# Layer 1's values as seven products of quarters, computed between key units 6 and 7

## The chip, the cores and the metric

One NeuronCore of a Trainium2 chip runs the whole kernel. The metric is the device time of one execution in microseconds (us), as a median of runs. TensorE (PE in the profile) multiplies matrices, VectorE (DVE), ScalarE (ACT) and GpSimd (POOL) work elementwise, SyncE (SP) issues most of the transfers, GpSimd the adding ones. Sixteen DMA engines carry the transfers of all queues.

## The reference

A two-layer decoder step: layer 0 is gated linear attention, layer 1 differential attention, each with an MLP. The prompt has 16 meta tokens and 1024 further ones, width 1024; beside it, 8 running sequences with 4096 past tokens each attend to a paged cache of keys and values. What the change touches is the projection of layer 1, `x @ w_in`, split into queries, keys and values:

```python
def diff_project(x, w_in, pos):
    B, T, _ = x.shape
    nq = DIFF_HEADS * 2 * DIFF_DH
    q, k, v = jnp.split(x @ w_in, [nq, 2 * nq], axis=-1)
    q = rope_partial(q.reshape(B, T, DIFF_HEADS, 2, DIFF_DH), pos)
    k = rope_partial(k.reshape(B, T, DIFF_HEADS, 2, DIFF_DH), pos)
    v = v.reshape(B, T, DIFF_HEADS, DIFF_DV)
    return q, k, v
```

Queries, keys and values have 1024 columns each. The values `v` of the prompt are an output (`v_rows_p`), and the attention reads them.

## The kernel before

Every large product is made of three matmuls in fp32r (`mm3`, L205 to L208): each operand is kept as a high part (`whi`, `XH`, cast by ScalarE) and a low part (`wlo`, `XL`, the difference, by GpSimd for weights in L194 and by VectorE for tokens in L203), and high x high, high x low and low x high are summed in one PSUM bank. The tokens lie transposed in `XH`/`XL`: halves `c` of 512 tokens, blocks `k` of 128 inner columns (eight of them, so a half of the inner size is four blocks).

The projection of layer 1 (loop at L1237) runs over 12 units `u` of 256 output columns (0 to 3 queries, 4 to 7 keys, 8 to 11 values) and, in each, over 4 steps `t2_` of two blocks of 128 tokens. A step is 48 matmuls of 256 columns into one bank (`mmt`); ScalarE copies the bank to `qo` (L1252), VectorE turns the first 16 of every 64 columns for queries and keys (L1260 to L1263), SyncE stores the result (L1269). The weights of a unit come through two `raw` buffers of 128 x 512 and two pairs of `whi`/`wlo` (pools `wrp` and `wsp`, two buffers each).

Woven into the same stretch is the paged decode of the 8 running sequences (generator `decode`): for each sequence 32 pages of keys and, one sequence later, 32 pages of values of 512 KB each through 10 buffers `pg`. Key pages are multiplied by the query (L942, three of four on VectorE and one on GpSimd) and summed (L943); value pages are multiplied on TensorE (L983, eight records a page). The softmax of a sequence (`soft`, from L948) stands between its key pages and its value pages; `v_end` (L994 to L999) ends it.

Between the units stand side steps: after unit 3 and unit 6 the residual `Y` (128 x 8192, one bank of on-chip memory for 1024 tokens) is scaled and gets its bias row (`alpha_row`, L1130 and L1128) and is stored to `xres`, after which `Y` is free; after unit 9 the keys and queries of the first two heads are loaded (`load_qk`), and `prep(0)` transposes them in the middle of the last unit, for the attention that follows.

Code is recorded in program order, and a scheduler then orders each engine's instructions by that order as a priority and by its own model of when an operand is ready; on the chip, each engine and each queue runs its list in order. `decode` has the lowest priority. `issue_after` ties an instruction behind another.

Layer 1's MLP, later in the kernel, already computes products by seven products of quarters (`UP_*`, `DOWN_*`); weight sums there are made by adding transfers from GpSimd's queue (L1620), on buffers `RW`.

## Time and profile before

| | us |
|---|---|
| median of 3 runs | 2798.05 |
| lowest and highest | 2793.52, 2802.12 |
| the profiled execution's own time | 2807.25 |
| its span, first to last instruction | 2805.4 |
| granted TensorE clock, mean | 0.991 |

| engine | busy, us | share of the span |
|---|---|---|
| PE | 2725.4 | 97% |
| PEld (weight load of TensorE) | 2237.5 | 80% |
| DVE | 1935.9 | 69% |
| ACT | 1107.1 | 39% |
| POOL | 1091.0 | 39% |

All traces are of one profiled execution. In a row of the time line stand the start, the duration, the engine, the line, the operation, out<-in with shapes, and in brackets the idle time before it and what ended that. A group's row has the line, engine, operation, out<-in, count, busy us and mean ns of one, then the engine's idle time before them. Matmuls overlap, so the time of one is read from the distance of starts, not from its duration.

### The profile page before, as it was taken

The page shows a single profiled execution, that of the slowest core. Times are in us where ns is not written, and L with a number is a line of the kernel's source. Part 1 is how long each engine was busy: PE and PEld are TensorE (multiplying, and loading weights), DVE is VectorE, ACT ScalarE, POOL GpSimd, SP SyncE. Part 2 cuts the span into 40 slices and gives each one's busy share as a digit, 9 for nine tenths or more (in the row PEclk, how much of TensorE's full clock was granted, in tenths as well). Part 3 has the DMA queues.
Part 4 walks back from the last instruction along what each step waited for, and adds up shares of the span by engine and source line. Part 5 has one row for each costly group of instructions (what it writes and reads, how often), then busy time and mean ns, then how long its engine had stood idle before and what let it go on. Part 6 is the DMA issues. An engine that isn't in the chain of part 4 may idle for free.

```text
span 2805.4 us, 52242 instructions
## 1 busy us (share of the span) xinstructions
PE 2725.4 (97%) x19849; PEld 2237.5 (80%) x19849; DVE 1935.9 (69%) x3011; ACT 1107.1 (39%) x2266; POOL 1091.0 (39%) x744
## 2 busy tenths in 40 slices
PE   8989999999999999999999999899999999999997
PEld 5867767987777777777798989777899889798985
DVE  5375363678787787777667730887647888978698
ACT  4324463152221222221242112777526546355553
POOL 2132112234344443434234312200026667686765
PEclk9999999999999999999999999999999999999999
DMA  7475545735798898888658995212044555564674
GB/s 237 164 242 207 202 154 184 262 97 184 284 333 320 310 351 302 331 319 306 250 173 312 363 368 169 64 55 79 31 126 90 103 139 113 134 133 104 140 179 112
DMA packets 275624, 562.81 MB, mean 201 GB/s; under 512 B 23510, under 2 KB 144412, under 8 KB 271276
## 3 DMA queue, kind: packets, MB, share of 16 engines
q1 hardware_dynamic: 256076, 522.75, 54.0%
q0 software_dynamic: 19296, 36.71, 8.1%
q8 instruction: 156, 2.56, 0.4%
q14 instruction: 96, 0.79, 0.1%
HBM read 533.00 MB, written 29.52 MB: 201 GB/s over the span
## 4 chain that ended last, share of the span: by engine, by line
PE 78%; DVE 9%; DMA 4%; ACT 4%; issue 3%; POOL 1%; SPq 0%; DVEq 0%; POOLq 0%; ACTq 0%
PE mmt L206 18%; PE mmt L207 18%; PE mmt L208 18%; PE smt L983 4%; PE axt L206 3%; PE axt L208 3%; PE axt L207 3%; PE smt L1359 2%; ACT as L1337 1%; DMA swt<-in_mlp_w 1%; DVE pg L942 1%; PE prt L1333 1%; PE axt L1354 1%; DVE XH L203 1%; DVE sc L943 1%
## 5 line engine op out<-in xcount | busy, mean ns | idle before, releaser
L194 POOL TENSOR_TENSOR wlo<-raw,whi 128x512 fp32r<-128x512 f32 x252 | 361.5, 1448 | 719.0 <-ACT whi L193 616.2
L206 PE MATMUL mmt<-whi,XH 128*128 128x256 f32 (+1 forms) x1760 | 524.2, 300 | 1.1 <-DVE ast L1335 0.9
L207 PE MATMUL mmt<-wlo,XH 128*128 128x256 f32 (+1 forms) x1760 | 522.8, 298 | 0.6 <-POOL wlo L194 0.6
L206 PE MATMUL mmt<-XH,whi 128*128 128x512 f32 (+1 forms) x1216 | 435.9, 360 | 3.4 <-DVE HL L203 1.8
L208 PE MATMUL mmt<-whi,XL 128*128 128x256 f32 x1536 | 432.6, 285 | 0.0
L208 PE MATMUL mmt<-XH,wlo 128*128 128x512 f32 (+1 forms) x1216 | 432.4, 356 | 0.2 <-POOL wlo L1622 0.2
L193 ACT CAST whi<-raw 128x512 fp32r<-128x512 f32 x252 | 150.4, 619 | 574.2 <-DMA raw<-in_mlp_w 172.9
L206 PEld LDWEIGHTS mmt<-whi,XH 128*128 128x128 f32 x1760 | 330.8, 189 | 39.6 <-issue 24.3
L943 DVE TENSOR_REDUCE sc<-pg 128x16 f32<-128x1024 f32 x256 | 308.2, 1211 | 69.7 <-POOL pg L942 67.2
L207 PEld LDWEIGHTS mmt<-wlo,XH 128*128 128x128 f32 x1760 | 332.6, 189 | 16.8 <-issue 5.8
L942 DVE TENSOR_TENSOR pg<-pg,qb 128x1024 f32<-128x1024 f32 x192 | 267.1, 1398 | 63.5 <-DMA pg<-in_cache_k 50.5
L207 PE MATMUL mmt<-XL,whi 128*128 128x512 f32 x768 | 306.7, 400 | 0.0
L208 PEld LDWEIGHTS mmt<-whi,XL 128*128 128x128 f32 x1536 | 288.6, 189 | 7.3 <-issue 6.8
L206 PEld LDWEIGHTS mmt<-XH,whi 128*128 128x128 f32 x1216 | 229.6, 189 | 46.9 <-issue 7.6
L942 POOL TENSOR_TENSOR pg<-pg,qb 128x1024 f32<-128x1024 f32 x64 | 163.0, 2548 | 249.3 <-DMA pg<-in_cache_k 139.8
L208 PEld LDWEIGHTS mmt<-XH,wlo 128*128 128x128 f32 x1216 | 229.9, 189 | 36.1 <-issue 3.3
L206 PE MATMUL mmt<-whi,HH 128*128 128x512 f32 x512 | 204.8, 401 | 5.6 <-DVE Y L1172 3.7
L208 PE MATMUL mmt<-whi,HL 128*128 128x512 f32 x512 | 203.9, 398 | 0.0
L207 PE MATMUL mmt<-wlo,HH 128*128 128x512 f32 x512 | 203.4, 397 | 0.0
L1622 POOL TENSOR_TENSOR wlo<-rw,whi 128x512 fp32r<-128x512 f32 x92 | 154.4, 1737 | 93.6 <-ACT whi L1621 90.4
L1622 POOL TENSOR_TENSOR wlo<-RW,whi 128x512 fp32r<-128x512 f32 x96 | 164.1, 1750 | 59.1 <-ACT whi L1621 59.0
L207 PEld LDWEIGHTS mmt<-XL,whi 128*128 128x128 f32 x768 | 145.3, 189 | 39.3 <-issue 8.0
(438 smaller groups left out, 5697.6 us busy)
## 6 DMA issues: line engine op xcount, KB each, us to landing
pg<-in_cache_k SPq DMA_DIRECT2D x256, 512.0 KB
pg<-in_cache_v SPq DMA_DIRECT2D x256, 512.0 KB
raw<-in_mlp_w SPq DMA_DIRECT2D x164, 256.0 KB
swt<-in_mlp_w SPq DMA_DIRECT2D x32, 1024.0 KB
rw<-in_mlp_w SPq DMA_DIRECT2D x116, 256.0 KB
RW<-in_mlp_w POOLq DMA_DIRECT2D x96, 256.0 KB, 5.7
swt<-in_gla_w_in SPq DMA_DIRECT2D x12, 1024.0 KB
swt<-in_diff_w_in SPq DMA_DIRECT2D x12, 1024.0 KB
```

The lines of the kernel that those rows point to most:

```text
L193: S.copy(hi[:, c], raw)
L194: G.tensor_tensor(lo[:, c], raw, hi[:, c].bitcast(F32), op=ALU.subtract)
L203: return eng.tensor_tensor(lo, src, hi.bitcast(F32), op=ALU.subtract)
L206: TE.matmul(ps, ah, bh, start=first, stop=False)
L207: TE.matmul(ps, ah, bl, start=False, stop=False)
L208: return TE.matmul(ps, al, bh, start=False, stop=last)
L942: eng.tensor_tensor(pg, pg, qb, op=ALU.mult)
L943: return V.tensor_reduce(sc[:, n, :], pg.rearrange("p (h d) -> p h d", d=64), op=ALU.add, axis=AX.X).ins
L983: m = TE.matmul(acc[i * TS : i * TS + 16, :256], w[r, n, :], pg[r, i * 256 : (i + 1) * 256], start=n == 0, stop=n == NPG).ins
L1333: TE.matmul(pss[m], qs[i][r, ts_], ks[j][r, x:y], start=i + j == 0, stop=i == 1)
L1359: TE.matmul(out, at, v, start=j == 0, stop=j == t + 1)
L1622: G.tensor_tensor(lo[:, k, :], t, hi[:, k, :].bitcast(F32), op=ALU.subtract)
```

## The change

The loop over units ends at 8. The values are computed by `v_rows`, which runs between unit 6 and unit 7, as seven products of quarters: tokens by halves `c` and inner size by halves `k`, weights by halves `k` and halves `u` of the 1024 value columns, each quarter 512 x 512. In the order 5, 1, 6, 2, 3, 4, 7 (`V_SEQ`), with A(c,k) for tokens and W(k,u) for weights, the factors are:

| product | tokens | weights |
|---|---|---|
| 5 | A(1,0) - A(1,1) | W(0,0) + W(0,1) |
| 1 | A(0,0) | W(0,0) |
| 6 | A(0,0) - the sum of 5 | the sum of 5 + W(1,1) |
| 2 | A(0,1) | W(1,0) |
| 3 | A(0,1) - the sum of 6 | W(1,1) |
| 4 | A(1,1) | the sum of 6 + W(1,0) |
| 7 | A(1,0) - A(0,0) | W(1,1) + W(0,1) |

A product is 4 tiles of 128 tokens, each 12 matmuls of 512 columns, alternately in banks `axt` and `mmt`. Token sums are formed by VectorE in a quarter of `Y` (`VX`) and split into one buffer `vtok`; weight sums are formed in another quarter of `Y` (`VW`), where a plain load is followed by an adding transfer, or an adding transfer goes onto the sum that stands there. The other two quarters of `Y` (`VA`, `VB`) hold running results. Product 1's result is stored, and product 2's is added onto it in DRAM by an adding store. The operands of a product are recorded after two tiles of the one before; those of product 5 after step 0 of unit 6 (`v_first`).

So that `Y` is free in time, the bias rows and the store to `xres` move from after unit 6 to after unit 4. The loads of the first two heads' keys and queries move from after unit 9 to behind the values, since `vtok` takes the place of their buffers; `prep(0)` stays in the middle of the last unit, which is now key unit 7.

```diff
-    rqp = er.enter_context(tc.tile_pool(name="rqp", bufs=2, side="right"))
+    vs = ExitStack()
+    vtok = vs.enter_context(tc.tile_pool(name="vtok", bufs=1, side="right")).tile([P, 2, 4, 512], F32R, name="vtok")
...
+    V_SEQ = (5, 1, 6, 2, 3, 4, 7)
+    VX, VW, VA, VB = (Y[:, 2048 * i : 2048 * (i + 1)].rearrange("p (k n) -> p k n", n=512) for i in range(4))
...
+        for j in (0, 2):
+            b = slice(j, j + 2)
...
+            if rest == ["run"]:
+                V.tensor_tensor(x, hi, x, op=ALU.subtract)
+                V.tensor_tensor(x, x, lo, op=ALU.add)
+            else:
+                h2, l2 = at(*rest[0])
+                V.tensor_tensor(x, hi, h2, op=ALU.subtract)
+                V.tensor_tensor(x, x, lo, op=ALU.add)
+                V.tensor_tensor(x, x, l2, op=ALU.subtract)
+            split(vtok[:, 0, b], vtok[:, 1, b], x)
...
+        for k in range(4):
...
+            t = VW[:, k] if len(terms) > 1 else wrp.tile([P, 512], F32, name="raw")
+            for q in terms:
+                if q != "run":
+                    if q == terms[0]:
+                        dma(t, src(q))
+                    else:
+                        nc.gpsimd.dma_start(t, src(q), accum_op=ALU.add)
+            S.copy(hi[:, k], t)
+            G.tensor_tensor(lo[:, k], t, hi[:, k].bitcast(F32), op=ALU.subtract)
...
+        for k in range(4):
+            mm3(ps, ah[:, k, ts_], al[:, k, ts_], bh[:, k], bl[:, k], k == 0, k == 3)
+        if i == 5:
+            S.copy(VB[:, t], ps)
+        elif i == 1:
+            S.copy(VA[:, t], ps)
+            dma(v_out(0, t, 0), VA[:, t])
+        elif i == 6:
+            V.tensor_tensor(ps, ps, VA[:, t], op=ALU.subtract)
+            V.tensor_tensor(VB[:, t], VB[:, t], ps, op=ALU.add)
+            S.copy(VA[:, t], ps)
+        elif i == 4:
+            V.tensor_tensor(VA[:, t], ps, VA[:, t], op=ALU.subtract)
+        else:
...
+            if i == 2:
+                S.copy(o, ps)
+                nc.gpsimd.dma_start(v_out(0, t, 0), o, accum_op=ALU.add)
+                return
+            V.tensor_tensor(o, ps, VB[:, t], op=ALU.add)
+            dma(v_out(int(i == 7), t, 1), o)
...
-    for u, t2_ in ((u, t) for u in range(12) for t in range(4)):
+    for u, t2_ in ((u, t) for u in range(8) for t in range(4)):
+        if (u, t2_) == (7, 0):
+            v_rows(v_now)
+            vs.close()
+            rqp = er.enter_context(tc.tile_pool(name="rqp", bufs=2, side="right"))
+            raws = [load_qk(0), load_qk(1)]
...
-        if (u, t2_) == (11, 2):
+        if (u, t2_) == (7, 2):
...
-        elif (u, t2_) == (6, 3):
+        elif (u, t2_) == (4, 3):
...
-        elif (u, t2_) == (9, 3):
-            raws = [load_qk(0), load_qk(1)]
+        elif (u, t2_) == (6, 0):
+            v_now = v_first()
```

Three places of the engines' lists. First SyncE, where the residual's store (`xres<-Y`, four pieces) frees `Y`. Before, its first two pieces in unit 7 (`L1123` loads rows of a bias, `L909` is a page's address):

```order
L1269 DMA out_k_rows_p<-qo 128x2x256
L909 TENSOR_LOAD ptab
L909 ISA x2
L1278 DMA xres<-Y 128x8x256
L1123 DMA ht<-in_ln_mlp_b 128x256
L1278 DMA xres<-Y 128x8x256
```

Now, in units 5 and 6, with product 5's four weight slabs (`Y<-in_diff_w_in`): around the third and fourth piece of the store, and then between unit 6's second and third store of keys:

```order
L1372 DMA xres<-Y 128x8x256
L1272 DMA Y<-in_diff_w_in 128x512
L1363 DMA out_k_rows_p<-qo 128x2x256
L1272 DMA Y<-in_diff_w_in 128x512
L1372 DMA xres<-Y 128x8x256
L1363 DMA out_k_rows_p<-qo 128x2x256
```

```order
L911 DMA pg<-in_cache_k 128x1024
L909 TENSOR_LOAD ptab
L909 ISA x2
L1363 DMA out_k_rows_p<-qo 128x2x256
L1272 DMA Y<-in_diff_w_in 128x512 x2
L1363 DMA out_k_rows_p<-qo 128x2x256
```

Two slabs (those whose columns of `Y` the first two pieces of the store cover, 0 and 2) are loaded right behind the third piece, the other two half a unit later. Before, the store stood two units later and nothing was loaded into `Y` behind it.

Second GpSimd, from the end of unit 6 to the last key page. `L942` is a page's product, `L974` and `L992` memsets of the decode, `wlo` a weight's low part. Before, with key unit 7's weights and the first of the values':

```order
L942 TENSOR_TENSOR pg<-pg,qb 128x1024
L194 TENSOR_TENSOR wlo<-raw,whi 128x512 x2
L942 TENSOR_TENSOR pg<-pg,qb 128x1024
L194 TENSOR_TENSOR wlo<-raw,whi 128x512
L974 MEMSET pg 32x1024
L194 TENSOR_TENSOR wlo<-raw,whi 128x512
L992 MEMSET pg 128x256
L942 TENSOR_TENSOR pg<-pg,qb 128x1024
L194 TENSOR_TENSOR wlo<-raw,whi 128x512 x6
```

Now, in one run (`wlo<-Y` are the slabs of a weight sum, for products 5 and then 6; `wlo<-raw` those of product 1; L1274 the adding transfers):

```order
L1274 DMA Y<-in_diff_w_in 128x512 x2
L942 TENSOR_TENSOR pg<-pg,qb 128x1024
L1276 TENSOR_TENSOR wlo<-Y,whi 128x512
L1276 TENSOR_TENSOR wlo<-raw,whi 128x512 x2
L1274 DMA Y<-in_diff_w_in 128x512 x2
L1276 TENSOR_TENSOR wlo<-Y,whi 128x512
L1274 DMA Y<-in_diff_w_in 128x512
L942 TENSOR_TENSOR pg<-pg,qb 128x1024
L1274 DMA Y<-in_diff_w_in 128x512
```

```order
L974 MEMSET pg 32x1024
L992 MEMSET pg 128x256
L1276 TENSOR_TENSOR wlo<-raw,whi 128x512 x2
L1276 TENSOR_TENSOR wlo<-Y,whi 128x512
L1274 DMA Y<-in_diff_w_in 128x512
L1276 TENSOR_TENSOR wlo<-Y,whi 128x512
L1274 DMA Y<-in_diff_w_in 128x512
L942 TENSOR_TENSOR pg<-pg,qb 128x1024
L1276 TENSOR_TENSOR wlo<-Y,whi 128x512 x2
```

Between the last three page products of the decode there now stand 8 low parts and 6 adding transfers, where 4 low parts stood.

Third VectorE, at the last key page (`L943` its sum, `L948` the first step of the softmax) and at the decode's end (`L999`). Before, behind the last rotation of key unit 7:

```order
L1263 TENSOR_TENSOR qo<-qo,qr 128x8x16
L943 TENSOR_REDUCE sc<-pg 128x16
L948 TENSOR_REDUCE mx<-sc 128x16
L999 COPY oT<-smt 128x4 x2
L952 TENSOR_REDUCE m_18529<-smt 16x1
```

Now, first at the last key page (`vtok` is product 6's token split), then at the decode's end (L1305 and L1309 are results of products 3 and 7, L1298 of product 4):

```order
L942 TENSOR_TENSOR pg<-pg,qb 128x1024
L943 TENSOR_REDUCE sc<-pg 128x16 x2
L948 TENSOR_REDUCE mx<-sc 128x16
L203 TENSOR_TENSOR vtok<-Y,vtok 128x1024
L1252 TENSOR_TENSOR Y<-XH_85,Y 128x1024
L203 TENSOR_TENSOR vtok<-Y,vtok 128x1024
```

```order
L1305 TENSOR_TENSOR qo<-mmt,Y 128x512
L999 COPY oT<-smt 128x4 x2
L1388 MEMSET cmask 128x320
L1480 TENSOR_TENSOR zoq<-oT 128x64
L1483 TENSOR_SCALAR zoq<-smt 128x64
L1305 TENSOR_TENSOR qo<-axt,Y 128x512
L1309 TENSOR_TENSOR qo<-Y,axt 128x512
L1305 TENSOR_TENSOR qo<-mmt,Y 128x512
```

Product 6's tokens stand behind the last key page, and product 7's results behind the last step of the decode.

More of the change, by code (lines that the diff above doesn't have):

```diff
@@ new lines, in v_weights @@
+    def v_weights(i):
+        terms = [q for q in DOWN_W[i] if q != "new"]
+        hi, lo = (wsp.tile([P, 2048], F32R, name=n).rearrange("p (k n) -> p k n", n=512) for n in ("whi", "wlo"))
+        for k in range(4):
+            src = lambda q: wd[512 * q[0] + k * P : 512 * q[0] + (k + 1) * P, 2048 + 512 * q[1] : 2560 + 512 * q[1]]
+            t = VW[:, k] if len(terms) > 1 else wrp.tile([P, 512], F32, name="raw")
[7 more added lines that the diff above has]
+            G.tensor_tensor(lo[:, k], t, hi[:, k].bitcast(F32), op=ALU.subtract)
+        return hi, lo
@@ new lines, in v_first, with v_rows @@
+    def v_first():
+        return v_tokens(V_SEQ[0]), v_weights(V_SEQ[0])
+    def v_rows(now):
+        n = 0
+        for at, i in enumerate(V_SEQ):
+            for t in range(4):
+                if t == 2 and at < 6:
+                    nxt = v_weights(V_SEQ[at + 1])
+                    nxt = v_tokens(V_SEQ[at + 1]), nxt
+                n += 1
+                v_tile(i, t, *now, axt() if n % 2 else mmt())
+                next(paged, None)
+            now = nxt
+    units, outs = {}, []
@@ L1267, in hybrid_step @@
             hs = slice(2 * (u % 4), 2 * (u % 4) + 2)
-            dst = A["k_rows_p" if u < 8 else "v_rows_p"][0, 0, pr, hs, :].rearrange("t h d -> t (h d)")
+            dst = A["k_rows_p"][0, 0, pr, hs, :].rearrange("t h d -> t (h d)")
         dma(dst.rearrange("(i p) n -> p i n", p=P), o)
```

36 lines of the change are left out of this document (27 added, 9 removed).

## The prediction

> **What bounds the kernel now.** I read the page first, for the engine that sets the end, then the stretch of layer 1's projection by windows, then rows of that stretch. From the page, the span, the slices of TensorE and of the DMA engines, the DMA queues and the chain by engine:
>
> ```profile
> span 2805.4 us, 52242 instructions
> PE   8989999999999999999999999899999999999997
> DMA  7475545735798898888658995212044555564674
> q1 hardware_dynamic: 256076, 522.75, 54.0%
> q0 software_dynamic: 19296, 36.71, 8.1%
> PE 78%; DVE 9%; DMA 4%; ACT 4%; issue 3%; POOL 1%; SPq 0%; DVEq 0%; POOLq 0%; ACTq 0%
> ```
>
> TensorE is on 78% of the chain that ended last, so time taken off TensorE counts, unless it comes back as a wait. The changed stretch is slices 21 to 25 (each 70 us). Its ends by ScalarE's copies of the finished tiles, which are the last of key unit 6, the last of key unit 7, and two neighbours and the end of value unit 11:
>
> ```profile
> 1608.16 0.59 ACT L1252 COPY qo<-mmt 128x512 f32<-128x512 f32 x1 [4.98 <-PE mmt L208]
> 1633.76 0.59 ACT L1252 COPY qo<-mmt 128x512 f32<-128x512 f32 x1 [5.12 <-PE mmt L208]
> 1721.64 0.59 ACT L1252 COPY qo<-mmt 128x512 f32<-128x512 f32 x1 [5.13 <-PE mmt L208]
> 1727.29 0.59 ACT L1252 COPY qo<-mmt 128x512 f32<-128x512 f32 x1 [5.06 <-PE mmt L208]
> 1752.04 0.58 ACT L1252 COPY qo<-mmt 128x512 f32<-128x512 f32 x1 [5.11 <-PE mmt L208]
> ```
>
> And the engines there (length, then PE, PEld, DVE, ACT, POOL busy, clock, DMA share, GB/s):
>
> ```profile
> 1560.00:1580.00 20.00, 20.00 (x186) 18.84 (x185) 14.15 (x23) 3.01 (x5) 7.97 (x5) 1.00 1.06 368
> 1608.00:1634.00 26.00, 26.00 (x246) 24.45 (x245) 23.47 (x32) 3.63 (x7) 8.44 (x6) 1.00 1.05 384
> 1634.00:1706.00 72.00, 71.59 (x693) 54.92 (x692) 8.10 (x18) 14.69 (x29) 14.37 (x13) 1.00 0.85 313
> 1706.00:1752.00 46.00, 46.00 (x391) 45.83 (x389) 4.11 (x10) 10.37 (x19) 10.19 (x10) 1.00 0.52 157
> ```
>
> TensorE never stands still, at clock 1.00. But the DMA engines are full up to 1634 (share 1.05) and at 0.85 until 1706: that is the paged decode, and the values' projection stands right on its tail.
>
> **Term 1: the matmuls.** Before, the values take 4 units of 192 matmuls of 256 columns, 768. One tile of 48 lasts 1727.29 - 1721.64 = 5.65 us, 0.118 us each: 90.4 us. Afterwards there are 7 products of 4 tiles of 12 matmuls of 512 columns, 336. Such a tile stands in layer 1's MLP, from its first matmul to the next tile's:
>
> ```profile
> 2240.60 0.40 PE L206 MATMUL axt<-whi,XH 128*128 128x512 f32 x1
> 2243.37 0.40 PE L206 MATMUL mmt<-whi,XH 128*128 128x512 f32 x1
> ```
>
> 2.77 us for 12, 0.231 each: 77.6 us. The saving is 12.8 us, all on TensorE's path. The decode's matmuls and key unit 7 keep their number.
>
> **Term 2: the first two products' weights.** This is the place that I fear most. Product 5 opens the stretch with a weight sum: a plain load of 4 slabs, an adding DMA onto each, ScalarE's high part, GpSimd's low part. The slabs lie in Y, free only once the residual is stored; SyncE's order in the section on the change therefore loads slabs 0 and 2 early and 1 and 3 only in unit 6. GpSimd then has, in order, what stands there. Its prices (low part; page product; adding DMA's issue), the decode's matmuls and the landing:
>
> ```profile
> L194 POOL TENSOR_TENSOR wlo<-raw,whi 128x512 fp32r<-128x512 f32 x252 | 361.5, 1448 | 719.0 <-ACT whi L193 616.2 <-DMA raw<-in_gla_w_in 28.9 <-PE mmt L208 19.5
> L942 POOL TENSOR_TENSOR pg<-pg,qb 128x1024 f32<-128x1024 f32 x64 | 163.0, 2548 | 249.3 <-DMA pg<-in_cache_k 139.8 <-DMA pg<-in_cache_v 46.4 <-PE mmt L208 22.7
> L1620 POOL DMA_DIRECT2D RW<-in_mlp_w x96 | 94.7, 1200 | 17.6 <-DMA RW<-in_mlp_w 16.9 <-issue 0.4 <-POOL wlo L1622 0.3
> RW<-in_mlp_w POOLq DMA_DIRECT2D x96, 256.0 KB, 5.7
> 1622.58 0.94 POOL L974 MEMSET pg<- 32x1024 f32 x1 [0.65 <-PE smt L983]
> 1624.72 0.30 POOL L992 MEMSET pg<- 128x256 f32 x1
> 1619.94 1.14 ACT L193 CAST whi<-raw 128x512 fp32r<-128x512 f32 x2
> 1638.65 0.56 PE smt L983 x8
> ```
>
> From unit 6's end at 1608.2: copy and high part 1.2; slab 0's low part 1.45; two low parts of product 1, 2.9, to 1613.7. Only now are slabs 1's and 3's adds issued (94.7/96 = 1.0 us of queue each); slab 1 lands 5.7 us later, 1619.4, and with 0.6 and 1.45 is ready at 1621.5. Then add, page product, add, two memsets, two low parts, slab 2's: 1.0 + 2.55 + 1.0 + 1.24 + 2.9 + 1.45, to 1631.6; add and slab 3's, 1634.1. By its order TensorE has then some 24 matmuls (5.5 us) and 3 pages of 8 records at 0.56 left: 1641. Without any wait it would be through at 1608.2 + 96 x 0.231 + 13 pages x 0.56 = 1637.7. So 3 us late. Next on GpSimd is the last key page.
>
> ```profile
> 1629.37 2.43 POOL L942 TENSOR_TENSOR pg<-pg,qb 128x1024 f32<-128x1024 f32 x1 [4.36 <-DVE qr L1262]
> 1636.29 1.21 DVE L943 TENSOR_REDUCE sc<-pg 128x16 f32<-128x1024 f32 x1
> 1637.53 1.08 DVE L948 TENSOR_REDUCE mx<-sc 128x16 f32<-128x528 f32 x1
> 1701.25 0.62 PE L983 MATMUL smt<-pg,sc 32*16 32x256 f32 x8
> ```
>
> VectorE's order has product 6's token split behind that reduction: 1634.1 + 1.0 + 2.55 + 1.2 + 1.1 + a split like L942's VectorE form (1.2) gives 1641.2, against 1637.7: 3.5 us late, in parallel with the above, not added to it. The adds' 5.7 us are from a stretch with DMA engines half empty; beside pages they land later. Bounds: 0 (GpSimd's 1.29 us forms, data early) and 3.5 + 6 (a landing twice as long) = 9.5. I take 6, halfway, since the DMA share at that place is 1.05.
>
> **Term 3: the decode's end.** The queues' rows give 54.0% x 2805.4 / 522.75 = 2.90 us of all 16 DMA engines for a plain MB, and 8.1% x 2805.4 / 36.71 = 6.19 for an adding one, 3.04 and 6.49 a MiB. Until the decode ends the change adds 5 MiB of adds (four weight quarters, one output quarter) and takes away 2.25 MiB of plain traffic (one more weight quarter, but unit 7's key stores and the first two heads' loads come later): 32.4 - 6.8 = 25.6 us, or 8.4 if an add costs what its bytes would. The stretch 1634 to 1706 has 15% of 72 us, 11 us, free. So the last pages come up to 15 us later. Before, they were issued at 1683 to 1684:
>
> ```profile
> 1683.18 0.95 SPq L911 DMA_DIRECT2D pg<-in_cache_v  x2
> ```
>
> Afterwards that is by 1699; with as long to land as an add's 5.7 it is 1705. TensorE used the last page's rows at 1701.25, 93 us after unit 6; its new order has it 576 units of 256 columns on instead of 557, so at about 1702, with term 2's delay 1708. Cover enough; bounds 0 and 6, I take 1. If it fails, VectorE holds product 7's results behind the decode's last copy (its order), and TensorE stops for want of banks.
>
> On the adds, the Trainium skill ("Collectives: The Full Stack", Part 3, on the bandwidth ceiling) says that the add in the DMA path costs no cycles of its own but needs two source reads, so such traffic runs at half rate. The rows above agree, 6.19 against 2.90 (2.1 times). By it the 25.6 us stand, not the 8.4.
>
> The busiest slice of the page and the busiest window I saw show 384 and 401 GB/s. The Trainium skill ("Perfetto Trace Analysis", the box on HBM above 100%) gives a core's 16 DMA engines about 435 GB/s in all. By it an estimated 8 to 13% would be free even where the share reads 1.05, term 3 would be nothing and term 2 nearer its 3.5; the trace shows no slice above 401, so I keep the shares.
>
> ```profile
> 1600.00:1620.00 20.00, 20.00 (x187) 18.85 (x186) 16.66 (x25) 3.54 (x7) 4.98 (x3) 1.00 1.05 401
> GB/s 237 164 242 207 202 154 184 262 97 184 284 333 320 310 351 302 331 319 306 250 173 312 363 368 169 64 55 79 31 126 90 103 139 113 134 133 104 140 179 112
> ```
>
> **Costed at nothing.** VectorE gains 28 token operations of 1024 columns (1.2 us, 34 us) and 24 of 512 for results: hidden in 1634 to 1706, where it works 8.10 of 72 us; before 1634 only the first six stand, in the place of the bias rows that moved two units forward. The residual's 4 MiB store moves with them into a full DMA stretch (1560 to 1580, share 1.06) and delays pages there as much as it frees later. The first heads' keys and queries are loaded after the values, 1 MiB a head, and used half a unit (11 us) later; that covers 3 us of transfer. ScalarE works under a fifth of the time there.
>
> **Sum.** -12.8 + 6 + 1 = -5.8 us. On the profiled run: span 2805.4 to 2799.6, its own time 2807.25 to 2801.5. That run lies 9.2 above the median of the runs shown, 2798.05; the forecast for the median is 2798.05 - 5.8 = **2792**.
>
> **Rivals.**
> - *Nothing waits.* Adds land while TensorE works on the other product; for it speaks layer 1's MLP, where seven products run on adds without a wait, at a DMA share of 0.46:
>
> ```profile
> 2240.00:2260.00 20.00, 20.00 (x91) 15.34 (x90) 19.12 (x18) 3.67 (x5) 9.01 (x7) 1.00 0.46 121
> ```
>
>   Waits of 1 us: 2798 - 12 = 2786.
> - *The decode's tail takes it.* Term 3 at its upper bound and term 2 in full: -12.8 + 6 + 6 = -1, 2797. For it: share 0.85 to 1.05; against: free buffers ahead.
> - *Slower: the sums' landing.* In the full DMA queue an adding slab lands not 5.7 but 12 us after its issue (four in a row at 6.49 us a MiB, shared half and half with pages: 13 us). Then product 5's slab 1, product 6's last slab and product 7's first, each behind the slab before it in the same buffer, are late by 6.3, some 2.5 and 6 more: -12.8 + 7 + 14.8 = +9, 2807. It decides from a landing of about 8 us: three chains, (12.8 - 7)/3 = 1.9 us each.
>
> That the change doesn't do what it says is excluded: TensorE's order holds the 336 matmuls.
>
> **Chances.** Forecast 0.40, nothing waits 0.25, decode's tail 0.15, slower by the landing 0.20. The two likeliest cases lie around 2786 to 2795. The range: 2782 (no wait, 1.3 below the saving for rounding and the runs' scatter) to 2808 (the slow case with 1 us), which leaves under 2 in 10 out. A measurement of this kernel tells 0.3% (8.4 us) from no change. Faster by more: nothing waits, and a quarter of the forecast, 0.35. Slower by more: most of the slow case and a little of the tail, 0.20. Within: 0.45.
>
> **What will show it.** Term 1: 0.23 us between 512-column matmuls of the values, 336 of them. Term 2: TensorE idle at the start of products 5 and 6, ended by GpSimd's low part or VectorE's split, some 6 us in all; the adding loads' landing time in the page's last part, near 6 us or near 12. Term 3: a wait for a cache page or for VectorE near product 7. Wrong I would be if the waits stood elsewhere: in unit 4 to 6, where the residual's store moves, or in unit 7, for the heads' loads.

## The result, and the profile after

| | us | |
|---|---|---|
| after, median of 10 runs | 2813.25 | 2805.68 to 2825.41 |
| before, median of 10 runs on the same chip | 2800.82 | 2793.17 to 2811.41 |
| ratio | 1.0053 | 95% interval 1.0038 to 1.0068 |
| forecast | 2792 | range 2782 to 2808 |

The kernel became slower by 0.5%, some 15 us by the ratio. The forecast was 6 us faster, and the time lies above its range. The profiled execution of after (2805.68) is the fastest of its ten, and it was 9.9 us ahead of that of before already at the last copy of query unit 3 (1517.9 against 1527.8). So the traces are compared by distances between the same events, not by their ends.

The page of after, the lines that answer to those of before:

```profile
span 2803.9 us, 51524 instructions
PE   8989999999999999999999989899999999999997
q0 software_dynamic: 22176, 41.95, 9.0%
```

Fewer instructions, and 41.95 MB in the queue of the adding transfers where 36.71 were. On TensorE one slice, the 24th (1612 to 1682 us, where the values now stand), falls from 9 to 8. The same from the last matmul of key unit 6 to the last 256- or 512-column matmul of the projection, first before, then after (length, PE, PEld, DVE, ACT, POOL busy, clock, DMA share, GB/s):

```profile
1607.90:1751.70 143.80, 143.39 (x1324) 125.01 (x1323) 35.68 (x57) 28.69 (x54) 33.10 (x28) 1.00 0.78 276
```

```profile
1595.86:1756.30 160.44, 142.21 (x927) 100.03 (x925) 93.23 (x103) 44.99 (x78) 87.34 (x64) 0.93 0.89 289
```

This stretch is called the block below. It grew by some 17 us although 397 fewer records run on TensorE; the granted clock fell to 0.93; VectorE works 57.5 us more and GpSimd 54.2 us more. From unit 3's last copy to the first matmul of the attention's loop it is 238.7 us before and 257.2 after, 18.5 more: the block's 17, some 4 at the attention's start, and -2 ahead of the block. By the end of the attention 15.6 remain, which agrees with the 15 of the ratio.

What TensorE waited for in that stretch (engine, tile, line, what released it: us in total, times, longest). Before it was a single wait of 0.4 us; after:

```profile
PE smt L954 <- DVE m L952: 7.3, 1, 7.3
PE axt L206 <- ACT whi L1275: 5.3, 2, 4.5
PE prt L1427 <- DVE ast L1429: 4.8, 2, 4.5
PE axt L207 <- POOL wlo L1276: 4.6, 2, 4.3
PE axt L1448 <- DVE as L1435: 3.4, 1, 3.4
```

Three stops stand in the block; the rows of `prt` and `as` belong to the attention's start. From the gaps between matmul starts the block divides so: 0.6 us of stops before and 20.3 after; matmuls further apart than at full speed, 5.9 before (page changes) and 13.5 after; the rest, 137.3 and 126.7. So **-10.6 of matmuls, +19.7 of stops, +7.6 of slow matmuls**. A stop is counted here by the distance of starts, some 0.4 us more than the wait in the list.

**First stop, 4.9 us, at product 5.** TensorE and ScalarE in the time line of after:

```profile
1595.86 0.27 PE L208 MATMUL mmt<-whi,XL 128*128 128x256 f32 x1
1602.49 0.80 PE L206 MATMUL axt<-whi,vtok 128*128 128x512 f32 x1 [4.51 <-ACT whi L1275]
```

```profile
1601.33 0.59 ACT L1347 COPY qo<-mmt 128x512 f32<-128x512 f32 x1 [1.74 <-DMA out_k_rows_p<-qo]
1601.82 0.62 ACT L1275 CAST whi<-Y 128x512 fp32r<-128x512 f32 x1
```

The high part that TensorE wants takes 0.62 us, but it stands on ScalarE behind the copy of unit 6's last tile, and that copy waits until a store has freed a `qo` buffer.

**Second stop, 4.65 us, a low part of product 1.** TensorE, GpSimd, SyncE and ScalarE of after:

```profile
1619.45 0.79 PE L207 MATMUL axt<-wlo,XH 128*128 128x512 f32 x1 [4.25 <-POOL wlo L1276]
```

```profile
1605.28 4.53 POOL L1276 TENSOR_TENSOR wlo<-raw,whi 128x512 fp32r<-128x512 f32 x2
1616.85 3.77 POOL L1276 TENSOR_TENSOR wlo<-raw,whi 128x512 fp32r<-128x512 f32 x2
```

```profile
1607.61 2.57 SPq L1272 DMA_DIRECT2D raw<-in_diff_w_in  x2
```

```profile
1613.80 0.62 ACT L1275 CAST whi<-raw 128x512 fp32r<-128x512 f32 x1 [9.81 <-DMA raw<-in_diff_w_in]
```

The tokens are plain (`XH`), so this is product 1, the product without sums, and it waits for the low part of its third slab. Its first two low parts take 4.53 us, not 2 x 1.45, and there are two `raw` buffers, so the loads of the third and fourth slab are issued only as these are done, the third's at 1607.6. That slab is there at 1613.8; GpSimd then has a page's product and two memsets in its list (1612.8 to 1618.2) before the low part, which ends at 1619.4. The adds of slabs 1 and 3 also stand behind the first two low parts, but slab 1's low part ends only at 1621.9, when TensorE is running again.

On VectorE, beside GpSimd's row from 1610.9 to 1621.9 (low parts, the page's product, memsets):

```profile
1611.96 10.98 DVE L1253 TENSOR_TENSOR Y<-Y,XL 128x1024 f32<-128x1024 f32 x2
1622.87 0.28 DVE L1357 TENSOR_TENSOR qo<-qo,qr 128x128 f32<-128x128 f32 x1
```

Two additions that take 1.2 us each elsewhere last 10.98. Behind these stands unit 6's last rotation (L1357), and SyncE, with the next pages in its list behind that rotation's store, waits too: in 1620 to 1626 the DMA engines are down to 0.36.

```profile
1620.00:1626.00 6.00, 6.00 (x22) 3.66 (x21) 5.97 (x5) 1.18 (x3) 2.74 (x3) 0.55 0.36 72
```

**Third stop, 7.7 us, in a decode's softmax.**

```profile
1645.05 6.76 DVE L1252 TENSOR_TENSOR Y<-XH,Y 128x1024 f32<-128x1024 f32 x1
1651.85 1.23 DVE L1253 TENSOR_TENSOR Y<-Y,XL 128x1024 f32<-128x1024 f32 x1
1653.13 0.27 DVE L952 TENSOR_REDUCE m<-smt 16x1 f32<-16x128 f32 x1
```

```profile
1645.16 3.13 POOL L1276 TENSOR_TENSOR wlo<-raw,whi 128x512 fp32r<-128x512 f32 x2
1647.62 3.10 POOL L1276 TENSOR_TENSOR wlo<-Y,whi 128x512 fp32r<-128x512 f32 x2
```

The small reduction (0.27 us) that TensorE's next matmul needs is queued on VectorE behind a token sum, and that takes 6.76 us for as long as GpSimd runs four low parts.

**The slow matmuls.** After each stop TensorE starts again at about half speed:

```profile
1655.01 0.63 PE L206 MATMUL axt<-whi,XH 128*128 128x512 f32 x1
1655.43 0.63 PE L207 MATMUL mmt<-wlo,XH 128*128 128x512 f32 x1
```

```profile
1654.00:1661.00 7.00, 7.00 (x21) 5.67 (x21) 3.34 (x6) 0.64 (x1) 0.00 (x0) 0.60 0.89 252
```

The distance is 0.42 to 0.43 us where it was 0.231, at a granted clock of 0.60 (0.55 after the first two stops). 24 such distances stand behind the three stops, and 8 more, next to a stop or a page, took 0.56 to 0.59 in place of 0.31 to 0.34.

### The profile page after: what moved, and what is told of

Same layout as the page of the kernel before. It is cut to its first block, busy times and chain, and to the rows that moved or that the text cites. A ratio compares the mean times of both kernels' runs of the same rounds, so it can differ in the third digit from the quotient of the medians.

```text
span 2803.9 us, 51524 instructions
## 1 busy us (share of the span) xinstructions
PE 2711.5 (97%) x19417; PEld 2204.7 (79%) x19417; DVE 1986.2 (71%) x3063; ACT 1121.3 (40%) x2286; POOL 1131.5 (40%) x776
## 3 DMA queue, kind: packets, MB, share of 16 engines
q0 software_dynamic: 22176, 41.95, 9.0%
## 5 line engine op out<-in xcount | busy, mean ns | idle before, releaser
L194 POOL TENSOR_TENSOR wlo<-raw,whi 128x512 fp32r<-128x512 f32 x236 | 341.5, 1462 | 623.0 <-ACT whi L193 552.1
L206 PE MATMUL mmt<-whi,XH 128*128 128x256 f32 (+1 forms) x1528 | 462.1, 304 | 3.1 <-DVE qo L1309 1.0
L207 PE MATMUL mmt<-wlo,XH 128*128 128x256 f32 (+1 forms) x1528 | 460.0, 302 | 0.0
L208 PE MATMUL mmt<-whi,XL 128*128 128x256 f32 (+1 forms) x1304 | 369.8, 287 | 0.0
L193 ACT CAST whi<-raw 128x512 fp32r<-128x512 f32 x236 | 140.5, 619 | 567.4 <-PE mmt L208 183.1
L943 DVE TENSOR_REDUCE sc<-pg 128x16 f32<-128x1024 f32 x256 | 308.4, 1212 | 70.3 <-POOL pg L942 67.8
L206 PEld LDWEIGHTS mmt<-whi,XH 128*128 128x128 f32 x1528 | 287.3, 188 | 38.4 <-issue 22.4
L942 DVE TENSOR_TENSOR pg<-pg,qb 128x1024 f32<-128x1024 f32 x192 | 267.4, 1400 | 59.1 <-DMA pg<-in_cache_k 47.0
L207 PEld LDWEIGHTS mmt<-wlo,XH 128*128 128x128 f32 x1528 | 288.2, 189 | 14.9 <-issue 3.8
L942 POOL TENSOR_TENSOR pg<-pg,qb 128x1024 f32<-128x1024 f32 x64 | 162.6, 2542 | 265.9 <-DMA pg<-in_cache_k 184.6
L208 PEld LDWEIGHTS mmt<-whi,XL 128*128 128x128 f32 x1304 | 244.5, 189 | 5.9 <-issue 4.2
```

The lines of the kernel that those rows point to most:

```text
L193: S.copy(hi[:, c], raw)
L194: G.tensor_tensor(lo[:, c], raw, hi[:, c].bitcast(F32), op=ALU.subtract)
L206: TE.matmul(ps, ah, bh, start=first, stop=False)
L207: TE.matmul(ps, ah, bl, start=False, stop=False)
L208: return TE.matmul(ps, al, bh, start=False, stop=last)
L942: eng.tensor_tensor(pg, pg, qb, op=ALU.mult)
```

## The experiments

All were timed in 5 rounds beside the kernel before. "Block" and "stops" are taken from each run's trace as above.

| run | ratio and interval | block, us | stops, us |
|---|---|---|---|
| before | | 143.8 | 0.6 |
| after | 1.0053 [1.0038, 1.0068] | 160.4 | 20.3 |
| e17_again, the same kernel | 1.0059 [1.0041, 1.0077] | 159.3 | 19.4 |
| e1_move_only | 1.0004 [0.9989, 1.0019] | 140.6 | 1.1 |
| e2_eight | 1.0009 [0.9995, 1.0023] | 145.6 | 1.3 |
| e3_no_adds | 1.0017 [1.0004, 1.0031] | 150.7 | 10.3 |
| e4_low_dve | 1.0032 [1.0015, 1.0049] | 154.6 | 17.4 |
| e18_no_adds_low | 1.0015 [1.0001, 1.0029] | 143.8 | 9.4 |
| e5_plain_over | 1.0067 [1.0051, 1.0084] | 165.0 | 23.8 |
| e14_small_adds | 1.0058 [1.0039, 1.0078] | 159.0 | 18.6 |
| e6_no_tokens | 1.0061 [1.0040, 1.0081] | 161.4 | 25.9 |
| e13_no_sums | 1.0010 [0.9995, 1.0024] | 147.6 | 11.8 |
| e7_soft_first | 1.0069 [1.0052, 1.0086] | 163.2 | 22.7 |
| e8_order | 1.0045 [1.0030, 1.0061] | 151.5 | 15.2 |
| e9_qt4 | 1.0087 [1.0071, 1.0103] | 165.1 | 27.4 |
| e10_adds_first | 1.0064 [1.0039, 1.0088] | 161.2 | 22.7 |
| e11_early | 1.0057 [1.0037, 1.0076] | 159.8 | 20.7 |
| e12_filler | 1.0085 [1.0069, 1.0100] | | |
| e15_after_u7 | 1.0020 [1.0007, 1.0032] | | 1.7 |
| e16_after_u7b | 1.0059 [1.0045, 1.0073] | | |

### The place and the moves alone

In the kernel before, the bias rows and the residual's store two units earlier:

```diff
-        elif (u, t2_) == (6, 3):
+        elif (u, t2_) == (4, 3):
```

> The kernel before with one part of the change alone: the residual's bias rows and its store move from behind unit 6 to behind unit 4. Differences are against the kernel before (the change is +15 us). Theory A (the stops of TensorE at the starts of products 5, 1 and 6 are the loss): 0, within 3 us, since TensorE does not wait for the residual. Rival R1 (the 4 MiB store in the full DMA stretch holds back pages and stores for good): +5 or more.

And the values at the change's place, but as eight plain products (c, k, u), without any sum; two products in a row share a weight quarter, so there are 16 low parts where the seven products have 28:

```diff
-    V_SEQ = (5, 1, 6, 2, 3, 4, 7)
+    V_SEQ = tuple((c, k, u) for u in range(2) for k in range(2) for c in range(2))
...
```

> The change with eight plain products of quarters in place of seven: same place between units 6 and 7, same 512 columns and banks, same move of the residual, no sums of tokens or weights, no adding transfers, 384 matmuls. Theory A (the sums' work on VectorE and GpSimd makes the stops): no stop over 2 us in the stretch; 384 x 0.231 = 88.7 us of matmuls against 90.4 before, so -2, within 4 us of before, some 15 below the change. Rival R2 (the place beside the decode's tail costs it, whatever the products): +8 or more.

Neither can be told from before. The eight products have no stop worth naming; their longest wait:

```profile
PE smt L983 <- DMA pg<-in_cache_v: 0.5, 1, 0.5
```

So the loss does not come from the place, the wider tiles or the moved store, but from what the seven products add: the sums, and 12 more high and low parts. The rest of the block without stops and slow matmuls is 138.1 here and 126.7 with seven products: 11.4 us for 48 matmuls, 0.231 each by the forecast is 11.1.

### Which of the sums

The adding loads left out:

```diff
-                        nc.gpsimd.dma_start(t, src(q), accum_op=ALU.add)
```

> The change without its 16 adding loads of weight slabs: each weight sum keeps only the term that stands there already, so four of the seven products have wrong weights; the adding store of product 2, all tokens' sums and all low parts stay. Rival B (the adding loads' landing and their load on the DMA engines are the loss): the stops shrink from 17 us to under 6, -8 us against before. Theory A (VectorE's token sums held while GpSimd works, the softmax queued behind them, ScalarE's copy behind a store of keys): the stop of 7.7 us before product 6 and that of 4.9 us at product 5 stay, only the 4.6 us at the sum's second slab goes, with its slow clock: +8 us.

The low parts on VectorE in place of GpSimd:

```diff
-            G.tensor_tensor(lo[:, k], t, hi[:, k].bitcast(F32), op=ALU.subtract)
+            V.tensor_tensor(lo[:, k], t, hi[:, k].bitcast(F32), op=ALU.subtract)
```

> The change with the 28 low parts of the values' weights on VectorE (some 0.69 us each by its other 512-column operations) in place of GpSimd (1.3 to 1.5 us). Theory A: with GpSimd free, VectorE's token sums take 1.2 us instead of up to 6.8, and the softmax behind them comes some 6 us earlier: the stop of 7.7 us falls under 3, that of 4.6 us under 2; about +3 us against before. Rival B (landing of the adding loads): unchanged, +15. Rival R3 (VectorE gets too much work, 28 more operations in front of the decode's): stops stay over 15 us, ended by VectorE, +12 or more.

Both edits at once:

> The change without its adding loads (four products wrong, as before) and with the values' low parts on VectorE: GpSimd has no work of the values left, VectorE keeps the token sums and gets the low parts. Each alone gained against the change, 10 and 6 us. Theory G2 (GpSimd's row, by its length and by holding VectorE, is what the stops hang on): stops under 5 us, -3 us against before or better. Rival L (TensorE's stops move on whatever is taken away, since the decode's pages pace the stretch): stops of 10 us or more, +3 or more.

Each takes off part of the loss: stops of 10.3, 17.4 and 9.4 in place of 20.3. The interval of e4 overlaps that of after, so its gain in time is not clear of noise. In e4 the four L1252 and four L1253 take 1.22 us each, where after has up to 6.76, as it should be if GpSimd's low parts held them. The softmax wait (`m`, L952) is gone from the list too; that alone would show little, since it is also gone in e3, e5 and e10, where the low parts stay on GpSimd. The first stop stays:

```profile
PE axt L206 <- ACT whi L1275: 6.0, 1, 6.0
PE axt L207 <- DVE wlo L1276: 3.4, 3, 2.0
```

The traces of e3 and e18 have one wait of 8.9 us more at the attention's start, for VectorE behind an operation of GpSimd that in after stands elsewhere. In e3:

```profile
1746.98 10.57 POOL L1482 TENSOR_TENSOR zoq<-zoq,mhalf 128x64 f32<-128x64 f32 x1 [3.69 <-DVE zoq L1481]
```

VectorE's list has the step that needs its result ahead of the attention's. These two runs pay that, and it hides some of what they save.

Is it the adds' traffic? The adds as plain loads over the first, from SyncE; then the adds kept, but on 64 of each 512 columns:

```diff
-                        nc.gpsimd.dma_start(t, src(q), accum_op=ALU.add)
+                        dma(t, src(q))
```

> The change with its 16 adding loads made plain loads from SyncE onto the same slabs (a slab then holds the last term instead of the sum, so four products have wrong weights). The chain load, second load, high part, low part stays, and so does the traffic in bytes; what goes is GpSimd's issue of the adds (1 us of its row each) and the second read of an adding transfer. Rival B (a sum is late because its second transfer must land behind the first): the stops stay, +10 to +15 us against before. Theory A2 (the adds sit in GpSimd's row between low parts and page products, and their double cost fills the DMA engines): the stops shrink as without the second loads, +5 or less.

```diff
-                        nc.gpsimd.dma_start(t, src(q), accum_op=ALU.add)
+                        nc.gpsimd.dma_start(t[:, :64], src(q)[:, :64], accum_op=ALU.add)
```

> The change with adding loads of 64 of the 512 columns (sums wrong in the others): GpSimd issues as many, in the same places, and every wait for them stays, but their traffic is an eighth, 0.5 MiB instead of 4. Rival B2 (the adds' traffic beside the pages, and their landing, make the stops): like leaving them out, +5 us or less against before. Theory A3 (their issue in GpSimd's row, which holds VectorE, makes the stops): stops over 15 us, +12 or more.

With an eighth of the bytes the adds land in 3.9 us (median) in place of 7.8, and the time is that of the full change, 1.0058 beside 1.0053 and 1.0059 in its two runs. So the adds' bytes and landing are not the cause. In e5 GpSimd issues no adds of slabs, and the time is not better either, 1.0067; there the second loads stand in SyncE's list, and TensorE waits 9.2 us at a page. What e3 takes away beyond both is the step itself, a second transfer onto each slab between load and high part, whichever engine issues it.

The token sums left out:

```diff
-        if not rest:
+        if True:
```

> The change without its token sums and their splits on VectorE and ScalarE: products 5, 6, 3 and 7 use the first quarter of their tokens as it stands (their results are wrong). All weight sums, adding transfers and low parts stay. Theory A (VectorE's two-operand sums, held by GpSimd, keep the softmax and product 5 and 6 waiting): the stop of 7.7 us at the softmax goes, that at product 5 falls from 4.9 to about 4 (ScalarE's copy behind a store stays), the 4.6 us at the low part stays: +6 us against before. Rival B (weights alone): stops unchanged, +13 or more.

With this edit and that of e3 together:

> The change without its adding loads and without its token sums and splits (as in the two runs that leave out one of them; four of seven products are wrong): seven products, their low parts and their results stay. If the matmuls are worth what was forecast (12.8 us) and the sums alone make the stops: no stop over 2 us, -10 to -13 us against before. Theory G (the two kinds of sums fill different engines, and either one alone is enough to make TensorE stop): both gone must give much more than the gains of leaving out one (10 us and nothing, against the change). Rival H (the stops come from the order of the block, not from the sums): stops over 10 us stay, 0 or slower.

Without token sums alone (e6) nothing is won: the softmax wait goes, and ScalarE's high parts (11.4 us) and pages (11.3) take its place.

```profile
PE axt L206 <- ACT whi L1275: 11.4, 2, 5.9
PE smt L983 <- DMA pg<-in_cache_v: 11.3, 7, 3.9
```

Without any sum (e13) the time is that of the eight products, 0.4% or 12 us below the change, though 48 matmuls fewer run than in e2: rest 127.6 us, but stops of 11.8, nearly all in two places:

```profile
PE mmt L206 <- DVE qr L1354: 5.7, 1, 5.7
PE smt L983 <- issue: 4.4, 1, 4.4
```

By the time line the first is a bank that a rotation holds on VectorE behind a late key page, at a DMA share of 1.04; the second a cache page whose load stands on SyncE behind loads of weights.

### One wait after another

The softmax ahead of the token sums, by a tie:

```diff
-        V.tensor_reduce(m1, ps[:16, :P], op=ALU.max, axis=AX.X)
+        softs.append(V.tensor_reduce(m1, ps[:16, :P], op=ALU.max, axis=AX.X).ins)
...
+                with tc.issue_after(softs[-1]) if V_SEQ[at + 1] == 6 else nullcontext():
```

> The change with one order more: VectorE's token sums for product 6 come behind the softmax step that the stop of 7.7 us waited for. Theory A: that stop falls under 2 us, product 6 starts some 3 us later in its place, where value pages lie between; +7 to +10 us against before instead of +15. Rival B (adds late): the stop moves to product 6's weights or tokens in full, +13 or more.

The products in the order 1, 5, 2, 6, 4, 3, 7, so that a plain product opens the block. Here the last two tiles of product 3 read product 7's tokens, since these are split before them.

```diff
-    V_SEQ = (5, 1, 6, 2, 3, 4, 7)
+    V_SEQ = (1, 5, 2, 6, 4, 3, 7)
```

> The change in the order 1, 5, 2, 6, 4, 3, 7 in place of 5, 1, 6, 2, 3, 4, 7: a product without sums opens the stretch, the slabs of each weight sum are loaded and added right behind the low parts of the sum before, and product 5's tokens are formed in unit 6. Same matmuls, transfers and sums in total. Theory A and rival B alike: the stop at product 5 (4.9 us) and that at its second slab (4.6 us) go, since 48 matmuls more lie ahead of them. Theory A: GpSimd's row is as long as before and still holds VectorE, so the softmax waits some 5 us: +5 us. Rival B (only the lead of the adds counts): no stop over 2 us, -8 us.

Four `qo` buffers in place of three, for the first stop:

```diff
-    qt = e.enter_context(tc.tile_pool(name="qt", bufs=3))
+    qt = e.enter_context(tc.tile_pool(name="qt", bufs=4))
```

> The change with four buffers for finished tiles (qo) instead of three. Theory C (the first stop is a chain that begins with ScalarE: its copy of unit 6's last tile waits for an earlier store of keys to land before a buffer is free, and product 5's high parts stand behind that copy; everything on GpSimd behind them, the adds of slabs 1 and 3 too, is late by the same time): the first stop falls from 4.9 to under 2 us, product 1's stop of 4.6 comes earlier or shrinks; +8 us against before in place of +15. Rival D (product 5 waits for its tokens on VectorE anyway): first stop over 4 us, ended by VectorE's split, +14.

Product 5's loads and adds (`vw_load`, the same two loads in a function of their own) ahead of the low parts:

```diff
+            with tc.issue_after(adds[3]) if i in (5, 1) else nullcontext():
                 G.tensor_tensor(lo[:, k], t, hi[:, k].bitcast(F32), op=ALU.subtract)
...
+        vw_load(5)
+        return v_tokens(5), v_weights(5)
```

> The change with one order more on GpSimd: the adds of product 5's four slabs are all issued ahead of the low parts of products 5 and 1 (before, two of them stand behind three low parts). Theory C: the adds of slabs 1 and 3 are issued some 8 to 10 us earlier than in the change against the end of unit 6, so the stop of 4.6 us in product 5 goes, with the slow clock behind it; the first stop stays: +7 us against before. Rival B (landing of 7.5 us beside full DMA engines is what counts): the first low parts now wait for those adds' data in turn, the stops only move to the start: +13 or more.

With four buffers, and the bias rows, product 5's loads and its tokens still earlier:

```diff
-        elif (u, t2_) == (4, 3):
+        elif (u, t2_) == (4, 1):
...
+        elif (u, t2_) == (5, 1):
+            vw_load(5)
+        elif (u, t2_) == (5, 3):
+            left5 = v_tokens(5)
```

> The two orders together (four qo buffers, adds first), with the bias rows half a unit earlier, product 5's slabs loaded and tokens formed in unit 5, and each next sum's transfers recorded right behind the low parts of the one before. Same matmuls, transfers and sums. Theory C: the first two stops under 2 us each, the softmax stop stays (product 6's tokens are where they were): +2 us against before, at best -5. Rival E (whatever is put forward, the same work stands in the same full DMA stretch and TensorE waits elsewhere): stops of 15 us or more in other places, +10.

e7 lost the softmax stop and got 5.2 us at the tokens' split; e10 lost the low part's and got 8.8 at a page; e11 kept waits of 3.9 and 4.7 us at the first operands and got 4.1 and 4.2 at a softmax and a page. e9 did not even lose its own. Unit 6's last copy is no longer held (1598.46, behind its matmuls), but the first stop is still 5.2 us: ScalarE's list has the token casts ahead of the high part, and these wait for VectorE's sums (rows of e9).

```profile
1602.21 1.04 ACT L202 CAST vtok<-Y 128x1024 fp32r<-128x1024 f32 x1 [3.16 <-DVE Y L1258]
1604.76 0.61 ACT L1275 CAST whi<-Y 128x512 fp32r<-128x512 f32 x1
```

So the `qo` buffer was not the only thing that held the first stop. Besides, in e9 product 1's loads came to stand on SyncE behind a page, whose buffer waited for this:

```profile
1612.84 6.35 DVE L942 TENSOR_TENSOR pg<-pg,qb 128x1024 f32<-128x1024 f32 x1
```

a page's product of 1.2 us held to 6.35, and the high parts of those loads cost TensorE another 10.4 us:

```profile
PE axt L206 <- ACT whi L1275: 15.6, 2, 10.4
```

Only the order that begins with a plain product (e8) shortened the block, by 9 us, with 15.2 of stops; its 1.0045 cannot be told from the ratio of the change.

### The clock

Twenty matmuls that compute nothing, ahead of product 6, inside the third stop:

```diff
+        if (i, t) == (6, 0):
+            for k in range(20):
+                TE.matmul(ps, XH[:, k % 8, 0:P], XH[:, k % 8, 0:512], start=True, stop=True)
```

> The change with 20 matmuls of 512 columns more, whose result nothing reads, ahead of product 6's first on TensorE, where the stop of 7.7 us stands. Theory F (the clock falls in a stop and costs again behind it: product 6's first 20 matmuls stand 0.43 us apart instead of 0.23): the fillers run inside the stop, the matmuls behind it stand 0.23 apart, the granted clock there is 1.0 instead of 0.6: 2 to 4 us below the change, +12 us against before. Rival (the slow spacing is the wait for operands, not the clock): the fillers cost nothing and change nothing, spacing 0.43, +15; if the stop were no longer than 4 us in most runs, they would add up to 4.6 us, +19.

```profile
1651.58 4.79 PE L1288 MATMUL axt<-XH 128*128 128x512 f32 x20
...
1664.10 0.39 PE L954 MATMUL smt<-c_ident,m 16*128 16x16 f32 x2 [2.06 <-DVE m L952]
...
1664.77 0.40 PE L207 MATMUL axt<-wlo,XH 128*128 128x512 f32 x1
1665.00 0.40 PE L208 MATMUL axt<-whi,XL 128*128 128x512 f32 x1
```

```profile
1660.00:1668.00 8.00, 5.94 (x26) 4.54 (x25) 5.79 (x8) 0.64 (x1) 3.12 (x4) 1.00 1.07 327
```

The wait that is left is 2.06 us, and behind it the matmuls stand 0.23 apart at clock 1.00, not 0.43 at 0.60. So the slow matmuls are the stops' consequence. In total nothing is won: the fillers take their own 4.6 us, and in the trace the block is as long as in after (160.1 us). The run's ratio, 1.0085, lies above that of after all the same; from unit 3's last copy to the attention its trace has 254.2 us, beside 257.2, so what made it slower lies elsewhere and is not known.

### Behind the key pages

The whole block moved behind key unit 7, where the last key page is through, with the first head's loads in page buffers:

```diff
-        if (u, t2_) == (7, 0):
-            v_rows(v_now)
...
+    raw0 = load_first()
+    v_rows(v_now)
+    head = head0[0]
```

> The change with the values' block behind key unit 7 instead of in front of it (its first operands form in unit 7, and the first head's keys and queries are loaded into cache page buffers and transposed inside product 7). By then the decode's key pages, which need VectorE, GpSimd and half of the page traffic, are through. All sums are as in the change. Theory J (the sums are late because VectorE, GpSimd and the DMA engines are still busy with key pages there): stops under 8 us in the block, and of the forecast's 12.8 us most comes out, less some 5 us for the attention, which now starts right behind the values: -5 us against before, within 5. Rival K (the chain of a sum, load, add, high part, low part, is too long for the 22 us of two products wherever it stands): stops over 15 us, +10 or more.

The same with the second head's loads as early, and five `qo` buffers:

```diff
-    raw0 = load_first()
+    raw0 = [load_first(0), load_first(1)]
```

> The run with the values behind unit 7, with its attention start mended: five qo buffers, and the second head's keys and queries also loaded into page buffers and transposed inside product 7. In the run before, the block itself had one stop of 1.7 us and the attention's start some 17 us of stops. Theory J (the block behind the key pages runs without stops; what was left is the start of the attention): stops at the start fall under 8 us, -4 us against before or better. Rival L (the stops only move on, whatever is mended): 15 us of stops again, +5.

In e15 the seven products run almost without a wait; their one stop (1.7 us by the starts) is for a page:

```profile
PE smt L983 <- DMA pg<-in_cache_v: 1.3, 1, 1.3
```

The sums are the same; what is missing is the work of the key pages and of a key unit beside them. The engines are no emptier for it: in 1640 to 1660 VectorE works 17.2 of 20 us (16.2 in after), GpSimd 11.7 (12.2), and the DMA share is 0.99 in both. But unit 7 then has 5.3 us of stops, and at the attention's start there are three more, two of them for the heads' loads and results that now stand directly ahead of it:

```profile
PE prt L1441 <- DVE qo L1309: 5.2, 1, 5.2
PE axt L1228 <- DMA rkm<-out_k_rows_p: 5.0, 1, 5.0
PE axt L1462 <- DVE as L1449: 4.1, 1, 4.1
```

It ends at 1.0020. Moving those loads earlier (e16) brought waits back in unit 7 (`qr`, 7.4 us) and at pages (6.5), and 1.0059. No version was faster than before.

### The same kernel again

> The change once more, beside the run above on the same chip. It should repeat +15 us against before, with stops of 15 to 25 us in the values' block (20 in the first trace). If the stops lie elsewhere than in the first trace, no single one of them is the cause.

```profile
PE smt L954 <- DVE m L952: 7.7, 1, 7.7
PE axt L206 <- ACT whi L1275: 5.9, 2, 5.7
PE axt L207 <- POOL wlo L1276: 4.4, 1, 4.4
```

The same three stops with about the same lengths: they belong to the program, not to one execution.

## Why the prediction was wrong, step by step

- **Term 1** (-12.8): right, a little large. The matmuls gave 10.6 against before and 11.4 against the eight products at the same place.
- **Term 2** (6, bound 9.5) is the step that failed: 19.7 of stops and 7.6 of slow matmuls, 27 us. Of the places, the start of product 5 was named; the second stop, for a low part of the plain product 1, and the third, in a softmax, were not. It failed for four reasons. (1) Low parts and token sums were priced alone, 1.45 and 1.2 us, and taken to run beside each other. They hold each other: by their groups in after a low part of `raw` takes 2.03 us on average, and the token sums 2.87 (L1252) and 3.65 (L1253). (2) "VectorE's order has product 6's token split behind that reduction" looked at the key page's reduction, and did not ask which reduction TensorE waits for: that of the softmax stands behind the token sums. (3) ScalarE's list was costed from slab 0's landing ("copy and high part 1.2"), not from the `qo` buffer that its copy waits for, nor from the token casts in its list, which hold it as long without that wait (e9). (4) The slow clock after a stop was not counted at all. The landing, which I feared most, was 7.8 us in the median of after's adds (9.8 at most) in place of 5.7, and mattered least (e14). The expectations of e3 and e8 put the second stop at product 5's second slab; by the rows it is product 1's third.
- **The upper bound** of term 2 was not one: it doubled the landing and left every duration on GpSimd and VectorE as it is alone. The 6 us are not halfway either: half of 9.5 is 4.75, and between 3.5 and 9.5 it would be 6.5; neither is near 27.
- **Small slips.** The lower end of the range, 2782, lies 3.3 us below "no wait", not 1.3. The 384 GB/s are a window's; the page's busiest slice shows 368, and slices of 9 us in the trace of before reach 407, above the 401 named. None of these bears on the outcome.
- **Term 3** (1): the cost is about right, no wait for a page's data shows in after, but the working was not. The last page is issued 182.2 us after unit 3's last copy, 156.0 before, and the decode ends 30 us later relative to unit 6, not "up to 15". The DMA work came out at 33 engine-us more (25.6 to 32.4 in the forecast), but the free 11 us that I set against it lay behind the last page. Before, up to the last page's issue and then to the attention, and after the same:

```profile
1527.80:1683.80 156.00, 155.59 (x1500) 136.32 (x1492) 93.93 (x137) 25.82 (x46) 44.52 (x28) 1.00 0.99 362
1683.80:1766.50 82.70, 77.66 (x656) 69.30 (x653) 15.29 (x48) 24.58 (x49) 29.93 (x19) 0.96 0.48 153
```

```profile
1517.90:1700.10 182.20, 164.99 (x1274) 127.62 (x1267) 149.51 (x157) 43.08 (x73) 82.05 (x58) 0.93 0.95 326
1700.10:1775.10 75.00, 65.75 (x450) 52.86 (x449) 28.18 (x82) 22.89 (x46) 35.98 (x24) 0.91 0.75 231
```

  Ahead of the last page the share is 0.99 and 0.95, with little to spare. The last page is used at 1718.3 in after, 38 us before the block ends: unit 7 behind the values is the cover.
- **Costed at nothing**: VectorE's 34 us of token sums "hidden in 1634 to 1706, where it works 8.10 of 72 us". Its share was free, its order was not: with the decode later, the small operations that TensorE waits for stood behind the long ones.
- **The rivals.** "Nothing waits" and "the decode's tail" fell. "Slower: the sums' landing" had the sign and, with 2807, lay nearest, at a chance of 0.20, but its mechanism is refuted: at the measured 7.8 us its own sum gives about 0, not +15, and e14 halves the landing without a gain. That its number came near is luck. The measured case was none of mine: engines that hold each other, and the clock behind it.

**What is shown and what is open.** Shown: the sums cost the 12 us between the change and e13, and neither the place (e1, e2) nor the adds' bytes do (e14); the three stops repeat (e17); leaving out the second transfer onto the slabs takes off half of the stops (e3, e18); away from the key pages the block has almost no stops (e15). That VectorE's long durations are GpSimd's doing rests on the overlaps in the traces and on e4. Not settled is why e13, with neither adds nor token sums, gains nothing over the eight products: its two waits account for 10 us. One candidate is that pages arriving at a share near 1.0 set the pace of this stretch, so that time saved on TensorE returns as waits; that fits e6 to e11, but e15's block runs almost without stops at shares of 0.71 to 1.05. Another is the seven products' own operands: 28 high and low parts in e13 where e2 has 16, with more weight loads in SyncE's list. Neither was tried by itself.

## What to carry to other kernels

In a stretch where several engines run in-order lists on each other's results, price an added operation beside its neighbours, from rows where the other engine is at work, and ask which short operation now stands behind it. Free busy time on an engine is no cover; the place in its list is. When removing one wait after another only moves them, as here in e7 and e9 to e11, look for a place without the rival work before counting on the time saved; here even that (e15) gave the saving back at the stretch's two ends.

## What the runs showed of the hardware

- **VectorE can wait for GpSimd.** An operation of VectorE that reads two operands in SBUF can last as long as GpSimd's elementwise row beside it: 10.98 us for two of 1.2, 6.76 for one. In after, between 1480 and 1800 us, the 24 page products and token operations of 1024 columns that had no operation of GpSimd beside them took at most 1.23 us; of the 29 that had an elementwise one or a memset, 13 took more than 1.3, the others 1.2 to 1.3. Before it showed already, in the same rotation:

```profile
1507.33 2.18 DVE L1263 TENSOR_TENSOR qo<-qo,qr 128x128 f32<-128x128 f32 x1
1515.50 0.27 DVE L1263 TENSOR_TENSOR qo<-qo,qr 128x128 f32<-128x128 f32 x1
```

  Reductions (L943, 1.21 us) were not stretched. The Trainium skill ("GPSIMD Engine Reference", 1. Specifications, the row on SBUF interfaces) says that they are shared with VectorE and that instructions with two SBUF inputs contend; the traces agree, and add the price here.
- **The clock halves after a stop.** After waits of 4.3 us and more the clock was 0.55 to 0.60 and the matmuls 0.43 apart; after one of 2.06 it stayed at 1.00. The Trainium skill ("TensorE: Matmul & The Clock Gate", Part 1) gives an idle window of about 3.4 us, after which the clock is half; the runs agree. That the penalty is under 1% of a span holds here too (7.6 of 2804 us), but it was over half of what the change could save.
- One elementwise power of GpSimd on 128 x 64 takes 10.6 us (L1482 in e3). VectorE's next step on its result, and all behind that in VectorE's list, waits for it (5.1 us in e3); a rotation beside it (L1355, 0.29 us) was not stretched.
